# Batched matrix product on one core: a fourth output buffer, stores queued one pair later, and another order of copies on VectorE

## The chip, the cores and the metric

The kernel runs on one core of a Trainium2 chip. The core has engines that run side by side and meet only through semaphores: TensorE (PE, with its weight loads as PEld) multiplies and transposes, VectorE (DVE) and ScalarE (ACT) copy results out of the accumulators, GpSimd (POOL) and SyncE (SP) here mostly issue transfers. Sixteen DMA engines move data between the device memory (HBM) and the core's memory (SBUF); accumulators lie in PSUM. The metric is the device time of one execution in microseconds. Smaller is better.

## The reference

```python
def setup_inputs():
    batch, m, k, n = 32, 512, 1024, 768
    return {"x": randn(batch, m, k), "weight": randn(batch, k, n)}   # float32

def reference(x, weight):
    return np.matmul(x, weight).astype(np.float32)
```

There are 32 independent products of a 512 x 1024 by a 1024 x 768 matrix. All inputs are read once and all outputs written once, in float32: 167.77 MB in, 50.33 MB out.

## The kernel before

**Tiling.** TensorE contracts over 128 partitions, so x must lie transposed: K on the partitions. Each batch is handled as four row tiles (`mt` 0 to 3) of 128 rows; each needs 8 steps over K (`ko`) with 768 output columns. Loads go through POOL's queue and turn float32 into bfloat16 on the way (`load_w`, L89; `load_x`, L94). A weight load is one batch, an x load holds two batches, a "pair": batches 1 and 2, 3 and 4, and so on to 29 and 30. Batch 0 and batch 31 stand alone; batch 0's x comes in float32 through SP's queue into the space of an output buffer (`x_first`, L55).

**Transposes.** For a pair, TensorE does eight groups (`g`) of four transposes (L153) into two alternating accumulators `pts`, and VectorE copies each group into `both`, the transposed x (`spread_pair`, L222, its copy on L233; the last pair uses two smaller copies, L231 and L232; the last batch L236). Semaphore `s_pt` counts groups transposed, `s_c` groups copied. From the third group on, TensorE waits until the accumulator that it will overwrite has been copied.

**Multiplies and evictions.** `multiply` (L129) runs one row tile. Row tiles 0 and 1 share one set of three accumulator banks, 2 and 3 the other (`pms`). Each half batch (`p` 0 or 1) is copied out by two engines: ScalarE takes bank 0 and half of bank 2 (L265, L268; semaphores `s_a`, `s_ap`), VectorE bank 1 and the other half of bank 2 (L279, L281; `s_d`, `s_dp`). An output pair is batches 2a and 2a + 1; the two fill one output buffer `outs` of 24 KB per partition, and one store of 3 MB writes it (`store`, L107). The waits on `s_a` and `s_d` in `pair_on_pe` (L159) keep a multiply from overwriting a bank that isn't copied out: the second row tile of a batch waits for VectorE's bank 1 of the half batch just before it, as VectorE's order then also guarantees bank 2 of the half before that.

**What sets the order.** Each engine's program is one list, written out by hand: `on_pe`, `on_dve`, `on_act`, `on_pool`, `on_sp`. Transfers issued on one queue are moved in the order of issue.
- POOL issues, in round `b` of its loop (L321): for odd `b` the x load of the pair after next (which waits on `s_pt` until the old contents are transposed), then the store of output pair (b - 3) / 2; then for every `b` the weights of batch b + 3 (waits on `s_mm` until batch b - 1 is multiplied). In round 28 it issues the last two of its stores, 12 and 13.
- SP waits for every load's landing in the order of issue (`landed`, L298) and hands it on through `s_wr` (weights) and `s_xr` (x), which TensorE takes (L157). After all loads it issues the store of pair 14 and four half stores for batches 30 and 31.
- VectorE: for an odd batch first the eight copies of the pair's transposes; then, for every batch, the evictions of its two halves. So the second half of an even batch is evicted before the next pair's copies.
- Before an output buffer is written again, ScalarE and VectorE wait for its store (`slot_free`, L241). With three buffers, that is the store of three pairs ago.
- At the end SP waits for its stores, POOL for its own, and POOL clears the semaphores (`clear_on_pool`, L350).

Of the kernel before, what the change touches and what calls it, by code (L numbers as in the profile page):

```python
# [12 lines left out]
def kernel(  # L13
# [7 lines left out]
    B, M, K = x.shape  # L21
# [3 lines left out]
    MT = M // P  # L25
# [3 lines left out]
    ROW = MT * N  # L29
    AHEAD = 3  # L30
    LATE = 4
    HELD = 3
    GROUPS = 2 * MT
    W_SLOTS, X_SLOTS, OUT_SLOTS = 4, 2, 3
    LOOPS = (B - 4) // W_SLOTS
    LOOPED = 2 * LOOPS

    pe, dve, act, pool, sp = nc.tensor, nc.vector, nc.scalar, nc.gpsimd, nc.sync
# [7 lines left out]
    def sbuf(name, shape, dtype):  # L46
        return nc.alloc_sbuf_tensor(name, shape, dtype).ap()
# [4 lines left out]
    both = [sbuf(f"xT{i}", [P, 2, JT, 2, H, 2], BF16) for i in range(MT)]  # L52
    outs = [sbuf(f"out{i}", [P, 2 * ROW], F32) for i in range(OUT_SLOTS)]
    one = sbuf("one", [P, ROW], F32)
    x_first = outs[2][:, :MT * K].rearrange("p (mo k) -> p mo k", mo=MT)  # L55
    pts = [nc.alloc_psum_tensor(f"pt{i}", [P, JT, P], F32).ap() for i in range(2)]
    pms = [
        [nc.alloc_psum_tensor(f"pm{s}{i}", [P, 512], F32).ap() for i in range(3)] for s in range(2)
# [4 lines left out]
    def sem(name):  # L63
        sems.append(nc.alloc_semaphore(name))
        return sems[-1]

    s_first, s_zero, s_ident = sem("s_first"), sem("s_zero"), sem("s_ident")
    s_w = [sem(f"s_w{i}") for i in range(W_SLOTS)]
    s_x = [sem(f"s_x{i}") for i in range(X_SLOTS)]
    s_wr, s_xr = sem("s_wr"), sem("s_xr")  # L70
# [10 lines left out]
    def pt_done(k):  # L81
        return GROUPS * (k + 2)
# [6 lines left out]
    def load_w(b):  # L89
        if b >= W_SLOTS:  # L90
            pool.wait_ge(s_mm, mm_done(b - W_SLOTS))
        pool.dma_start(out=ws[b % W_SLOTS], in_=w_view[b]).then_inc(s_w[b % W_SLOTS], 16)  # L92

    def load_x(k):  # L94
        if k >= X_SLOTS:
            pool.wait_ge(s_pt, pt_done(k - X_SLOTS))
        slot = xs[k % X_SLOTS]
        if 2 * k + 1 == B - 1:
            pool.dma_start(out=slot[:, :MT], in_=x_view[B - 1]).then_inc(s_x[k % X_SLOTS], 16)
        else:  # L100
            pool.dma_start(out=slot, in_=pair_view[k]).then_inc(s_x[k % X_SLOTS], 16)  # L101
# [5 lines left out]
    def store(eng, a, sem):  # L107
        copied(eng, out_done(2 * a + 1) - 1)
        eng.dma_start(out=two_view[a], in_=outs[a % OUT_SLOTS]).then_inc(sem, 16)  # L109

    def store_half(b, p):
        src = one if b == B - 2 else outs[(b // 2) % OUT_SLOTS]
        half = slice(p * N2, (p + 1) * N2)
        copied(sp, 2 * b + p)
        sp.dma_start(out=out_view[b, :, half], in_=src[:, half]).then_inc(s_fin, 16)
# [106 lines left out]
    def spread_pair(k, g):  # L222

        pt = pts[g % 2].bitcast(BF16).rearrange("p j (b i r) -> p j b i r", b=2, r=2)
        tile, half = both[g // 2], g % 2
        if 2 * k + 2 == B - 2:

            rows = tile[:, 1].rearrange("p j h i r -> p j (h i r)").rearrange(
                "p j (m r) -> p j m r", r=2
            )  # L230
            dve.tensor_copy(tile[:, 0, :, half], pt[:, :, 0])  # L231
            return dve.tensor_copy(rows[:, :, half::2, :], pt[:, :, 1])  # L232
        return dve.tensor_copy(tile[:, :, :, half].rearrange("p b j i r -> p j b i r"), pt)  # L233
# [7 lines left out]
    def slot_free(eng, b):  # L241
        a = b // 2
        if a >= OUT_SLOTS and b % 2 == 0 and b < B - 2:
            eng.wait_ge(s_st[a % OUT_SLOTS], 16 * (a // OUT_SLOTS))
        if b == B - 1:
            eng.wait_ge(s_st[a % OUT_SLOTS], 16 * (a // OUT_SLOTS))

    def pieces(b, p, i):

        pm = pms[p][i]  # L250
        if b >= B - 2:
            dst = one if b == B - 2 else outs[(b // 2) % OUT_SLOTS]
            at = p * N2 + 512 * i
            return [(dst[:, at:at + 512], pm)]
        mine = outs[(b // 2) % OUT_SLOTS][H * (b % 2):H * (b % 2 + 1)]
        starts = [p * N2 + h * ROW + 512 * i for h in range(2)]
        return [(mine[:, at:at + 512], pm[H * h:H * (h + 1)]) for h, at in enumerate(starts)]

    def out_on_act(b, p):
        j = 2 * b + p  # L260
        if p == 0:
            slot_free(act, b)
        act.wait_ge(s_mm, 2 * j + 1)
        for piece in pieces(b, p, 0):
            last = act.copy(*piece)  # L265
        last.then_inc(s_a, 1)
        act.wait_ge(s_mm, 2 * j + 2)
        act.copy(*pieces(b, p, 2)[0]).then_inc(s_ap, 1)  # L268

    def out_on_dve(b, p):  # L270
        j = 2 * b + p
        if p == 0:
            slot_free(dve, b)
        dve.wait_ge(s_mm, 2 * j + 2)
        if b >= B - 2:
            dve.tensor_copy(*pieces(b, p, 1)[0]).then_inc(s_dp, 1)  # L276
            return
        for piece in pieces(b, p, 1):
            last = dve.tensor_copy(*piece)  # L279
        last.then_inc(s_d, 1)  # L280
        dve.tensor_copy(*pieces(b, p, 2)[1]).then_inc(s_dp, 1)  # L281

    def on_dve():
        for b in range(B):
            if b == 0 or b % 2:
                spread = {0: spread_first, B - 1: spread_last}.get(b)
                for g in range(MT if b == B - 1 else GROUPS):
                    dve.wait_ge(s_pt, (0 if b == 0 else pt_done(b // 2 - 1)) + g + 1)
                    (spread(g) if spread else spread_pair(b // 2, g)).then_inc(s_c, 1)
            for p in range(2):  # L290
                out_on_dve(b, p)

    def on_act():
        for b in range(B):
            for p in range(2):
                out_on_act(b, p)

    def landed(what, i):  # L298

        slots, ready = what  # L300
        sp.wait_ge(slots[i % len(slots)], 16 * (i // len(slots) + 1))
        sp.sem_inc(ready, 1)

    def on_pool():
        load_w(0)
        pool.memset(ident, 0.0).then_inc(s_zero, 1)
        pool.wait_ge(s_zero, 1)
        pool.affine_select(
            out=ident,
            in_=ident,  # L310
            compare_op=mybir.AluOpType.not_equal,
            fill=1.0,
            base=0,
            pattern=[[-1, P]],
            channel_multiplier=1,
        ).then_inc(s_ident, 1)
        load_x(0)
        load_w(1)
        load_w(2)
        load_x(1)  # L320
        for b in range(B):  # L321
            if b % 2 and b + AHEAD + 1 < B:
                load_x((b + AHEAD) // 2)
            if b % 2 and 2 < b < B - HELD - AHEAD:
                a = (b - 3) // 2
                store(pool, a, s_st[a % OUT_SLOTS])
            if b + AHEAD < B:
                load_w(b + AHEAD)
            if b == B - LATE:
                for a in (b // 2 - 2, b // 2 - 1):  # L330
                    store(pool, a, s_st[a % OUT_SLOTS])

    def on_sp():
        w, x = (s_w, s_wr), (s_x, s_xr)
        for what, i in ((w, 0), (x, 0), (w, 1), (w, 2), (x, 1)):
            landed(what, i)
        for b in range(B):
            if b % 2 and b + AHEAD + 1 < B:
                landed(x, (b + AHEAD) // 2)
            if b + AHEAD < B:  # L340
                landed(w, b + AHEAD)
        store_half(B - 2, 0)
        store(sp, B // 2 - 2, s_fin)
        store_half(B - 2, 1)
        store_half(B - 1, 0)
        store_half(B - 1, 1)
        sp.sem_inc(s_zero, 1)
        sp.wait_ge(s_fin, 80).then_inc(s_fin, -80)
# [10 lines left out]
    with tc.tile_critical():  # L359
        sp.dma_start(x_first, x_view[0]).then_inc(s_first, 16)  # L360
        on_pool()
        on_pe()
        on_dve()
        on_act()
        on_sp()
        clear_on_pool()
# [30 lines left out]
```

## Time and profile before

| | us |
|---|---|
| median of 3 runs | 515.88 |
| lowest and highest | 515.14, 516.1 |
| the profiled execution | 515.67 |
| its span, first to last instruction | 513.5 |
| PE busy | 430.2 (84%) |
| DVE busy | 209.6 (41%) |
| ACT busy | 110.2 (21%) |
| mean granted TensorE clock | 0.962 of full speed |

The views of the profile used here: the page's rows of busy tenths (one digit per fortieth of the span); the waits, with total, number and longest; the timeline, where a line gives start, duration, engine, source line, operation and in brackets the idle time before it with what ended it; the list of DMA issues, with size and time from issue to landing; and windows, which give each engine's busy time in a stretch and the share of time in which the DMA engines were busy. That share can come out a little over 1, as packets overlap. "L157" is line 157 of the kernel; "PEq" is TensorE's sequencer, "SPq" SP's.

A batch's multiplies take 10.35 us when TensorE waits for nothing. One eviction of half a bank takes VectorE 0.69 us, one copy of a transposed group 0.69, and ScalarE's copy 0.58.

### The profile page before, as it was taken

What the parts mean: (1) busy time and instruction counts of PE and PEld (TensorE: products, weight loads), DVE (VectorE), ACT (ScalarE), POOL (GpSimd) and SP (SyncE); (2) the same over time, 40 slices, a digit from 0 to 9 for tenths busy, and PEclk for the clock granted to TensorE, in tenths of its full rate; (3) what the DMA queues carried; (4) which work ended last, traced back from release to release, by engine and by line L of the source; (5) the groups of instructions that cost most, each with busy time, mean ns of one, the idle gap of its engine ahead of it and who ended that gap; (6) DMA issues with size and microseconds to landing.
All of it is one profiled execution on the core that took longest, in us unless ns stands there. A gap on an engine that the chain in (4) does not pass through costs nothing. (4 is left out here: it accounts for less than half of the span.)

```text
span 513.5 us, 6063 instructions
## 1 busy us (share of the span) xinstructions
PE 430.2 (84%) x2528; PEld 280.2 (55%) x2576; DVE 209.6 (41%) x332; ACT 110.2 (21%) x189; POOL 33.7 (7%) x68
## 2 busy tenths in 40 slices
PE   0889898998789789897878988788988879888995
PEld 0666565656456465554645655464565646556663
DVE  0463534535353353532534335263153632536331
ACT  0012223131122112222112221212213122121311
POOL 3001010101001010010100101001010010010000
PEclk9999999899998889999889999999899898898999
DMA  8999999999999999999999999999999999999995
GB/s 254 212 216 221 220 208 221 336 217 319 234 229 326 219 335 218 241 311 222 333 217 266 291 218 333 219 285 269 220 335 216 301 252 224 334 213 220 370 426 245
DMA packets 9803, 135.40 MB, mean 264 GB/s; under 512 B 1088, under 2 KB 1088, under 8 KB 1600
## 3 DMA queue, kind: packets, MB, share of 16 engines
q0 software_dynamic: 8928, 126.88, 96.1%
q1 hardware_dynamic: 864, 8.39, 4.1%
q8 instruction: 5, 0.08, 0.1%
q14 instruction: 6, 0.05, 0.0%
HBM read 167.77 MB, written 50.33 MB: 425 GB/s over the span
## 5 line engine op out<-in xcount | busy, mean ns | idle before, releaser
L134 PE MATMUL pm<-w,xT 128*128 128x256 bf16 (+1 forms) x2000 | 338.8, 328 | 32.8 <-PEq L157 29.9
L134 PEld LDWEIGHTS pm<-w,xT 128*128 128x128 bf16 x2048 | 202.2, 99 | 168.0 <-issue 40.8
L279 DVE COPY out<-pm 64x512 f32<-64x512 f32 x120 | 82.6, 689 | 252.4 <-PE pm L134 251.5
L265 ACT COPY out<-pm 64x512 f32<-64x512 f32 (+1 forms) x122 | 70.7, 580 | 300.6 <-PE pm L134 299.9
L153 PE MATMUL pt<-ident,x 128*128 128x128 f32 x496 | 87.3, 326 | 32.6 <-DVE xT L233 30.0
L153 PEld LDWEIGHTS pt<-ident,x 128*128 128x128 f32 x496 | 73.7, 210 | 45.6 <-DVE xT L233 39.3
L233 DVE COPY xT<-pt 128x1024 bf16<-128x1024 bf16 x112 | 73.5, 688 | 14.5 <-PE pt L153 13.8
L268 ACT COPY out<-pm 64x512 f32<-64x512 f32 (+1 forms) x62 | 35.8, 578 | 89.2 <-PE pm L134 89.2
L281 DVE COPY out<-pm 64x512 f32<-64x512 f32 x60 | 41.2, 686 | 0.0
L101 POOL DMA_DIRECT2D x<-in_x_dram x15 | 8.0, 532 | 274.0 <-PE pt L153 273.8
L92 POOL DMA_DIRECT2D w<-in_weight_dram x32 | 17.2, 538 | 125.6 <-PE pm L134 124.6
L153 PE MATMUL pt<-ident,out 128*128 128x128 f32 x32 | 6.9, 371 | 12.7 <-DMA out<-in_x_dram 12.5
L153 PEld LDWEIGHTS pt<-ident,out 128*128 128x128 f32 x32 | 5.3, 207 | 14.1 <-issue 12.5
L216 DVE CAST xT<-pt 128x256 bf16<-128x256 f32 x16 | 6.0, 441 | 14.4 <-PE pt L153 14.0
L109 POOL DMA_DIRECT2D out_dram<-out x14 | 7.5, 536 | 1.4 <-DVE out L281 1.3
L276 DVE COPY out<-pm 128x512 f32<-128x512 f32 x2 | 1.4, 692 | 9.0 <-PE pm L134 9.0
L276 DVE COPY one<-pm 128x512 f32<-128x512 f32 x2 | 1.4, 692 | 7.7 <-PE pm L134 7.7
L231 DVE COPY xT<-pt 128x512 bf16<-128x512 bf16 x8 | 3.4, 422 | 1.1 <-PE pt L153 0.9
L232 DVE COPY xT<-pt 128x512 bf16<-128x512 bf16 x8 | 3.3, 415 | 0.0
L236 DVE COPY xT<-pt 128x1024 bf16<-128x1024 bf16 x4 | 2.6, 684 | 0.2 <-PE pt L153 0.2
L265 ACT COPY one<-pm 128x512 f32<-128x512 f32 x2 | 1.2, 585 | 4.0 <-PE pm L134 4.0
L268 ACT COPY one<-pm 128x512 f32<-128x512 f32 x2 | 1.2, 585 | 4.0 <-PE pm L134 4.0
(8 smaller groups left out, 2.7 us busy)
## 6 DMA issues: line engine op xcount, KB each, us to landing
w<-in_weight_dram POOLq DMA_DIRECT2D x32, 1536.0 KB, 41.2
out_dram<-out POOLq DMA_DIRECT2D x14, 3072.0 KB, 36.5
x<-in_x_dram POOLq DMA_DIRECT2D x15, 2048.0 KB, 29.6
out_dram<-out SPq DMA_DIRECT2D x1, 3072.0 KB, 13.0
out<-in_x_dram SPq DMA_DIRECT2D x1, 2048.0 KB, 11.4
out_dram<-one SPq DMA_DIRECT2D x2, 768.0 KB, 9.3
out_dram<-out SPq DMA_DIRECT2D x2, 768.0 KB, 4.3
x<-in_x_dram POOLq DMA_DIRECT2D x1, 1024.0 KB, 23.2
```

The lines of the kernel that those rows point to most:

```text
L92: pool.dma_start(out=ws[b % W_SLOTS], in_=w_view[b]).then_inc(s_w[b % W_SLOTS], 16)
L101: pool.dma_start(out=slot, in_=pair_view[k]).then_inc(s_x[k % X_SLOTS], 16)
L109: eng.dma_start(out=two_view[a], in_=outs[a % OUT_SLOTS]).then_inc(sem, 16)
L134: last = pe.matmul(pm[bank][:, at:at + size], xT[:, ko // 2, :, ko % 2], w[:, ko, off:off + size], start=(ko == 0), stop=(ko == KT - 1),)
L153: last = pe.transpose(pts[g % 2][:, i, :], rows, ident)
L216: last = dve.tensor_copy(xT[:, 2 * (g % 2) + j].rearrange("p (h i) r -> p r h i", h=2), pt[:, 2 * j:2 * j + 2].rearrange("p r (i h) -> p r ...
L231: dve.tensor_copy(tile[:, 0, :, half], pt[:, :, 0])
L233: return dve.tensor_copy(tile[:, :, :, half].rearrange("p b j i r -> p j b i r"), pt)
L265: last = act.copy(*piece)
L268: act.copy(*pieces(b, p, 2)[0]).then_inc(s_ap, 1)
L279: last = dve.tensor_copy(*piece)
L281: dve.tensor_copy(*pieces(b, p, 2)[1]).then_inc(s_dp, 1)
```

## The change

Three things are done together.

First, there are four output buffers in place of three, and POOL issues the store of output pair (b - 5) / 2, in place of (b - 3) / 2, in an odd round b: each store stands one pair later among the loads. Rounds up to 25 issue stores 0 to 10 (before: 0 to 11), and after the last weights POOL issues stores 11, 12 and 13 (before: 12 and 13). A buffer's reuse moves by a pair as well. Batch 0's x uses the space of the fourth buffer, and the last batch uses the fourth too.

Second, VectorE defers the second half's eviction of an even batch until it has made the copies of the next pair's transposes.

Third, SP only hands on the weights' landings. ScalarE waits for an x load's landing between its two halves of each even batch and raises `s_xr`. The wait and the raising are one call in `landed` now.

```diff
-    HELD = 3
+    HELD = 4
     GROUPS = 2 * MT
-    W_SLOTS, X_SLOTS, OUT_SLOTS = 4, 2, 3
+    W_SLOTS, X_SLOTS, OUT_SLOTS = 4, 2, 4
...
-    x_first = outs[2][:, :MT * K].rearrange("p (mo k) -> p mo k", mo=MT)
+    x_first = outs[3][:, :MT * K].rearrange("p (mo k) -> p mo k", mo=MT)
...
     def on_dve():
         for b in range(B):
             if b == 0 or b % 2:
                 spread = {0: spread_first, B - 1: spread_last}.get(b)
                 for g in range(MT if b == B - 1 else GROUPS):
                     dve.wait_ge(s_pt, (0 if b == 0 else pt_done(b // 2 - 1)) + g + 1)
                     (spread(g) if spread else spread_pair(b // 2, g)).then_inc(s_c, 1)
-            for p in range(2):
-                out_on_dve(b, p)
+                if b:
+                    out_on_dve(b - 1, 1)
+            out_on_dve(b, 0)
+            if b % 2 or b == B - 1:
+                out_on_dve(b, 1)

     def on_act():
         for b in range(B):
-            for p in range(2):
-                out_on_act(b, p)
-
-    def landed(what, i):
+            out_on_act(b, 0)
+            if b % 2 == 0:
+                landed(act, (s_x, s_xr), b // 2)
+            out_on_act(b, 1)
+
+    def landed(eng, what, i):
         slots, ready = what
-        sp.wait_ge(slots[i % len(slots)], 16 * (i // len(slots) + 1))
-        sp.sem_inc(ready, 1)
+        eng.wait_ge(slots[i % len(slots)], 16 * (i // len(slots) + 1)).then_inc(ready, 1)
...
             if b % 2 and b + AHEAD + 1 < B:
                 load_x((b + AHEAD) // 2)
-            if b % 2 and 2 < b < B - HELD - AHEAD:
-                a = (b - 3) // 2
+            a = (b - 5) // 2
+            if b % 2 and 0 <= a < B // 2 - 1 - HELD:
                 store(pool, a, s_st[a % OUT_SLOTS])
             if b + AHEAD < B:
                 load_w(b + AHEAD)
             if b == B - LATE:
-                for a in (b // 2 - 2, b // 2 - 1):
+                for a in range(B // 2 - 1 - HELD, B // 2 - 2):
                     store(pool, a, s_st[a % OUT_SLOTS])

     def on_sp():
-        w, x = (s_w, s_wr), (s_x, s_xr)
-        for what, i in ((w, 0), (x, 0), (w, 1), (w, 2), (x, 1)):
-            landed(what, i)
         for b in range(B):
-            if b % 2 and b + AHEAD + 1 < B:
-                landed(x, (b + AHEAD) // 2)
-            if b + AHEAD < B:
-                landed(w, b + AHEAD)
+            landed(sp, (s_w, s_wr), b)
```

## The prediction

> **What bounds the kernel now.** I read the page first, then TensorE's waits, then the DMA landings of one cycle, then the last 60 us.
>
> ```profile
> DMA  8999999999999999999999999999999999999995
> HBM read 167.77 MB, written 50.33 MB: 425 GB/s over the span
> ```
>
> The 16 DMA engines are busy in all but the first and the last of 40 slices. Next, what TensorE waits for:
>
> ```profile
> PE pt L153 <- DVE xT L233: 30.0, 35, 1.9
> PE pm L134 <- PEq L157: 29.9, 13, 3.6
> ```
>
> Two waits share 60 us: transposes held by VectorE's copies (L233), and multiplies held by the "weights are in" semaphore (taken at L157). One pair shows how they alternate:
>
> ```profile
> 212.67 1.11 PE L153 MATMUL pt<-ident,x 128*128 128x128 f32 x8
> 215.64 1.35 PE L153 MATMUL pt<-ident,x 128*128 128x128 f32 x8 [1.87 <-DVE xT L233]
> 217.18 1.34 PE L153 MATMUL pt<-ident,x 128*128 128x128 f32 x8 [0.19 <-DVE xT L233]
> 218.71 1.35 PE L153 MATMUL pt<-ident,x 128*128 128x128 f32 x8 [0.19 <-DVE xT L233]
> 220.11 10.35 PE L134 MATMUL pm<-w,xT 128*128 128x256 bf16 x62
> ```
>
> The next batch then starts at 233.78, after 3.33 us of waiting for weights. The cycle's issues are an x load at 191.25, a store at 191.79, and weights at 192.31 and 201.76; they took, to landing:
>
> ```profile
> x<-in_x_dram POOLq DMA_DIRECT2D x1, 2048.0 KB, 27.7
> out_dram<-out POOLq DMA_DIRECT2D x1, 3072.0 KB, 34.4
> w<-in_weight_dram POOLq DMA_DIRECT2D x1, 1536.0 KB, 41.1
> w<-in_weight_dram POOLq DMA_DIRECT2D x1, 1536.0 KB, 39.0
> ```
>
> Issue plus duration gives landings at 218.95, 226.2, 233.4 and 240.8; the next x load (220.35 + 30.7) lands at 251.05. So transfers finish strictly in order of issue: a store takes the queue 7.25 us, a weight load 7.3, an x load 9.7 to 10.3, together 31.5 to 32 us per pair. The weights that landed at 233.4 are those TensorE got at 233.78. TensorE by itself needs 28.0 us per pair (transposes began at 31.09 and 59.13, before the queue caught up). DMA is the bound of the steady part, TensorE's waits are its shadow.
>
> The end is different. The last weights (issued 454.54) land at 481.8, 16 us before TensorE needs them; from 455.49 TensorE runs on without waiting for a load, to 508.4. Meanwhile the engines have stores 12 to 14 (numbered by pair) and four half stores of 768 KB. The last halves, issued at 503.99 and 509.12, took
>
> ```profile
> out_dram<-out SPq DMA_DIRECT2D x1, 768.0 KB, 5.2
> out_dram<-out SPq DMA_DIRECT2D x1, 768.0 KB, 3.3
> ```
>
> and the engines' load in that stretch (PE, PEld, DVE, ACT, POOL, clock, DMA share, GB/s):
>
> ```profile
> 490.00:500.00 10.00, 9.46 (x60) 6.53 (x61) 3.87 (x6) 1.75 (x3) 0.00 (x0) 1.00 1.01 432
> 500.00:505.00 5.00, 5.00 (x33) 3.05 (x32) 0.69 (x1) 1.17 (x2) 0.00 (x0) 1.00 0.82 349
> 505.00:508.00 3.00, 2.95 (x20) 1.77 (x19) 0.00 (x0) 0.58 (x1) 0.00 (x0) 1.00 0.66 272
> 508.00:513.50 5.50, 0.32 (x2) 0.00 (x0) 0.69 (x1) 0.58 (x1) 0.00 (x0) 0.86 0.36 146
> ```
>
> Only here does DMA run short of work: the last half waits for TensorE and lands alone at 512.4; 1.1 us of closing steps follow.
>
> **The change part by part.** *VectorE's order.* The transposes' copies no longer stand behind three evictions of 0.69 us. Of the 1.87 us stall the ordinary 0.19 stays: 1.68 us off each of 15 pairs, 25 us in all. The deferred evictions now hold TensorE's second multiply of the next batch (it waits for `s_d`). Here the copies end at 220.78; two evictions (1.39 us) would end at 222.17; the second multiply begins a quarter of 10.35 us after 220.11, at 222.7. Margin 0.5 us, so nothing is added; were it missed, the overrun would lie in front of a load wait anyway. In the steady part what comes late next is the same weights: TensorE arrives 1.7 us sooner and waits 5.0 us instead of 3.3. Worth there: nothing. In the last pair and the last batch nothing waits for loads, so TensorE's own end gains 1.92 - 0.19 (last pair) + 0.43 - 0.19 (last batch) = 2.0 us.
>
> *Store a pair later.* Bytes and transfers stay the same. With 11 instead of 12 stores ahead of them the loads from the third cycle on land 7.25 us earlier: the weights awaited at 455.17 at 447.9, the last ones at 474.6. TensorE's end becomes 508.4 - 7.25 - 2.0 = 499.1. Store 11 now follows the last weights, with 12 and 13, on POOL's queue; POOL passes only load issues (0.53 us each) with it, and nothing waits for those. Does the queue run dry early, without the store at 67.39? The x load that before went out at 95.68 goes out near 91; the work then queued ends at 113.7 (77.22 + 36.5) - 7.25 = 106.4. 15 us of backlog: no.
>
> *ScalarE hands on x loads' ends.* 16 semaphore waits move from SP to ScalarE, between its two evictions of an even batch; ScalarE idles 2.0 us there (rows of L265). Behind the wait stands the second eviction. x loads are issued two pairs ahead and land 25 to 31 us later. The tightest is the first: it lands at 25.7 (3.06 + 22.6), and ScalarE asks for it at 26.7, when the first evictions are done. Later ones have 2 us (the second lands at 50.4, asked for near 52.5) and more. Cost: nothing; were one late, TensorE would wait for that load itself.
>
> *Fourth buffer, later reuse.* A slot is free as long after its store as before (both move by a pair). The last batch now waits for store 11, due at 481.9, at about 491: nothing.
>
> *The sum.* After 474.6 the queues hold stores 11 to 14 and four halves. Check the rate on before: store 12 landed at 489.2 (455.08 + 34.1); two stores and three halves at 7.25 and 1.82 (a quarter) make 20.0 and an end at 509.2; measured 503.99 + 5.2 = 509.2. So the last-landing engine had no gap until then, and only the last half came loose: 512.4 against 509.2 + 1.8 = 511.0. Changed kernel: 474.6 + 4 x 7.25 + 4 x 1.82 = 510.9, the same by the other way round. TensorE's way, 499.1 + 0.76 to issue + 3.3, ends at 503: 8 us inside. So the span ends 1.35 us earlier: 512.15; with the 2.17 us between span and profiled time (515.67) this is 514.3. The profiled run stands 0.2 us under the median of 515.88, inside the runs' 0.96 us.
>
> Bounds of that gain. Upwards, if the mean engine decides and not the last: idle over the last windows is 5 x 0.18 + 3 x 0.34 + 5.5 x 0.64 = 5.4 us; less 1.1 closing and 1.5 latency of the last transfer (3.3 - 1.8) leaves 2.8. Downwards: POOL's queue and SP's now share the engines from 481 to 511, not only from 491 to 497. The window 490 to 500 (432 GB/s, two queues) against 480 to 490 (431, mostly one) says zero cost; one 1.6% below over 30 us would take 0.5. If POOL's stores end last, clearing the semaphores comes behind them: at most another closing, 0 to 1.1 us. I take 1.35, as it rests on landings of the last engine, and a semaphore needs all 16.
>
> [...]
>
> **The rivals.** (B) *No measurable change.* The filled gap is returned by the shared queues (0.5) and the late clear (up to 1.1): 515.0 to 516.0. For it: the bytes are the same, 97% of the span is already transfer, and an engine's odd delay (x loads vary by 0.6 us) weighs as much as the gain. Against: none of these costs shows in the 490 to 500 window.
>
> (C) *Slower.* Place: the closing 30 us, where two queues hold work on all engines at once and large and small packets alternate. At 4.5% loss of rate the 1.35 us are gone, at 8% (2.4 us) the kernel takes 516.7, slower by 0.2%. Before shows this mixture for only 6 us, where it costs nothing; that is the case against.
>
> (D) *TensorE's savings show.* Were transfers not the bound, 25 us would come off, to 490. Against: the landings, 7.3 us apart without a gap.
>
> **How the numbers follow.** 0.2% is 1.03 us, about what a measurement here can tell from no change. Forecast 0.60 (own range 512.8 to 514.8), B 0.30, C 0.08, D 0.02. Predicted is the forecast's 514.3. Low end 512.8 (gain 2.8); high end 516.5, which takes in B and part of C. Faster 0.60 + 0.02, same 0.30, slower 0.08.
>
> **What would show it.** TensorE's wait for L233 falls from 30.0 to under 8 us, its wait at L157 rises to about 55 (11 times 5). The first store goes out near 91 us; the last weights land near 474.6; TensorE ends near 499. The last half, issued near 500, takes some 11 us to land, and DMA share stays above 0.95 up to 508. A last landing at 509 to 511 confirms the sum. Wrong would be: a DMA share that dips between 500 and 508 with TensorE done (the rings had more slack than landings tell), landings more than 7.6 us apart at the end (rival C), or a `s_d` wait of over 0.3 us per pair in TensorE's rows.

## The result and the profile after

| | before | changed |
|---|---|---|
| median of 5 runs each | 515.44 us | 513.64 us |
| lowest and highest | 514.68, 516.1 | 513.3, 514.01 |
| profiled execution, its span | 515.67, 513.5 | 514.01, 512.2 |

The ratio is 0.9964 with a 95% interval of 0.9949 to 0.9978: the change takes 0.2 to 0.5% off. The spans of the two profiled executions differ by 1.3 us, as the sum had it; the medians differ by 1.8. In the experiments below, many more runs give the same size: the span's median is 513.0 us in 33 runs of the kernel before and 511.8 in 12 runs with the later stores alone.

First TensorE's waits in the changed kernel (total, number, longest, in us):

```profile
PE pm L134 <- PEq L157: 40.2, 13, 5.2
PE pt L153 <- DVE xT L233: 9.5, 42, 0.3
```

The wait for VectorE's copies fell from 30.0 to 9.5 us and its longest from 1.9 to 0.3. The wait for weights rose from 29.9 to 40.2. One cycle of the timeline shows both at once:

```profile
130.94 10.56 PE L134 MATMUL pm<-w,xT 128*128 128x512 bf16 x64 [2.69 <-PEq L157]
141.34 1.11 PE L153 MATMUL pt<-ident,x 128*128 128x128 f32 x8
142.76 1.35 PE L153 MATMUL pt<-ident,x 128*128 128x128 f32 x8 [0.30 <-DVE xT L233]
144.29 1.35 PE L153 MATMUL pt<-ident,x 128*128 128x128 f32 x8 [0.19 <-DVE xT L233]
145.82 1.35 PE L153 MATMUL pt<-ident,x 128*128 128x128 f32 x8 [0.18 <-DVE xT L233]
147.01 10.56 PE L134 MATMUL pm<-w,xT 128*128 128x512 bf16 x64
162.75 0.59 PE L134 MATMUL pm<-w,xT 128*128 128x512 bf16 x1 [5.18 <-PEq L157]
```

From the first transposes to the first multiply it is 5.7 us (before: 7.4), and what was won is waited for at the next weights.

The last weights go out at 445.12 and the last half store at 502.09 (timelines of POOL and SP); the issues with their durations to landing:

```profile
445.12 0.53 POOL L92 DMA_DIRECT2D w<-in_weight_dram  x1 [9.34 <-PE pm L134]
...
502.09 0.33 SPq L115 DMA_DIRECT2D out_dram<-out  x1
```

```profile
w<-in_weight_dram POOLq DMA_DIRECT2D x1, 1536.0 KB, 29.5
...
out_dram<-out SPq DMA_DIRECT2D x1, 768.0 KB, 9.0
```

So the last weights land at 474.6 and the last output at 511.1: the forecast's 474.6 and 510.9. The half that took 3.3 us alone now takes 9.0, behind others. The windows of the end (the columns before the last three are busy times of engines; then clock, DMA share and GB/s):

```profile
490.00:500.00 10.00, 10.00 (x65) 6.32 (x64) 2.66 (x5) 1.76 (x3) 0.00 (x0) 1.00 1.02 435
500.00:505.00 5.00, 1.28 (x8) 0.51 (x6) 0.69 (x1) 0.58 (x1) 0.00 (x0) 1.00 0.95 404
505.00:508.00 3.00, 0.00 (x0) 0.00 (x0) 0.00 (x0) 0.00 (x0) 0.00 (x0) 0.51 0.95 397
508.00:512.20 4.20, 0.00 (x0) 0.00 (x0) 0.00 (x0) 0.00 (x0) 0.00 (x0) 0.50 0.16 66
```

Where the DMA engines were busy 0.82 and 0.66 of the time, they are now busy 0.95, with TensorE done at 501.3. From 490 to 500, with two queues at work, they moved 435 GB/s, against 432 before: no price for sharing shows. In finer windows the share falls before the last landing:

```profile
507.00:508.00 1.00, 0.00 (x0) 0.00 (x0) 0.00 (x0) 0.00 (x0) 0.00 (x0) 0.50 0.80 332
508.00:509.00 1.00, 0.00 (x0) 0.00 (x0) 0.00 (x0) 0.00 (x0) 0.00 (x0) 0.50 0.41 172
```

The engines do not finish together: of the 16 landings that the trace has for the last store, the first stands at 508.0 and the last at 511.1 us (before: 512.2 and 512.4).

The page's chain of waits does not tell this. It still reads, for the changed kernel:

```profile
PE pm L134 9%; PE pt L153 1%; DVE xT L231 0%; DVE xT L232 0%; DVE xT L236 0%; DVE out L276 0%
```

It follows instructions back from the last one issued, and the last store's issue does hang on TensorE. That the store then stood in a queue is not in it. The experiments below ask which of the two ends the kernel.

### The profile page after: what moved, and what is told of

Same layout as the page of the kernel before. It is cut to its first block, busy times and chain, and to the rows that moved or that the text cites. A ratio compares the mean times of both kernels' runs of the same rounds, so it can differ in the third digit from the quotient of the medians.

```text
span 512.2 us, 6109 instructions
## 1 busy us (share of the span) xinstructions
PE 437.9 (85%) x2576; PEld 278.8 (54%) x2576; DVE 206.8 (40%) x332; ACT 110.2 (22%) x189; POOL 33.7 (7%) x68
## 5 line engine op out<-in xcount | busy, mean ns | idle before, releaser
L134 PE MATMUL pm<-w,xT 128*128 128x256 bf16 (+1 forms) x2048 | 356.2, 337 | 40.2 <-PEq L157 40.2
L134 PEld LDWEIGHTS pm<-w,xT 128*128 128x128 bf16 x2048 | 205.8, 101 | 186.2 <-issue 61.5
L233 DVE COPY xT<-pt 128x1024 bf16<-128x1024 bf16 x112 | 72.2, 687 | 61.0 <-PE pt L153 61.0
L153 PE MATMUL pt<-ident,x 128*128 128x128 f32 x496 | 80.0, 302 | 10.5 <-DVE xT L233 9.5
L153 PEld LDWEIGHTS pt<-ident,x 128*128 128x128 f32 x496 | 69.2, 209 | 21.8 <-DVE xT L233 17.4
L236 DVE COPY xT<-pt 128x1024 bf16<-128x1024 bf16 x4 | 2.6, 688 | 5.2 <-PE pt L153 5.2
```

The lines of the kernel that those rows point to most:

```text
L134: last = pe.matmul(pm[bank][:, at:at + size], xT[:, ko // 2, :, ko % 2], w[:, ko, off:off + size], start=(ko == 0), stop=(ko == KT - 1),)
L153: last = pe.transpose(pts[g % 2][:, i, :], rows, ident)
```

## The experiments

The theory: transfers in order of issue set the pace throughout. Before, the last half store came loose from that queue, as it waited for TensorE; the change closes this gap, and the copies' order is hidden. The main rival: TensorE's chain still ends the kernel, and the gain is its shorter path.

**One part at a time.** Only VectorE's order:

```diff
-            for p in range(2):
-                out_on_dve(b, p)
+                if b:
+                    out_on_dve(b - 1, 1)
+            out_on_dve(b, 0)
+            if b % 2 or b == B - 1:
+                out_on_dve(b, 1)
```

> Only VectorE's order is changed; stores and SP are those of the kernel before. My theory: transfers set the pace up to the last weights, so TensorE's saved 25 us vanish in waits for weights, but behind the last such wait (the weights that land at 455.2) TensorE gains 2.0 us, the last half store is issued near 507.1 instead of 509.1, and the end is the later of that plus 3.3 us (510.4) and the engines' backlog (511.0): 0.3 to 1.4 us less than before (the throttle may take some). So either part alone would fill the gap at the end. Rival: the gain is the stores' alone, this order is worth nothing: no difference (within 0.3 us).

Measured: 514.76 us against 514.97, ratio 0.9987 (0.9975 to 0.9998); span 512.8. The last half was issued at 508.35 in place of 509.12 and landed alone:

```profile
508.35 0.33 SPq L115 DMA_DIRECT2D out_dram<-out  x1
```

```profile
out_dram<-out SPq DMA_DIRECT2D x1, 768.0 KB, 3.3
```

That is 0.8 us earlier, within the expected range of 0.3 to 1.4 but short of its best. Behind the last wait for weights TensorE's stalls and gaps shrank by 2.5 us, but the multiplies right after this wait took 12.24 us where the kernel before took 10.56, and so took 1.7 back. (A stretch of 3.4 us at half clock would do this, an estimate from the eleven stretches of this length in the trace of the kernel before; the mean granted clock was 0.945 here and 0.962 there.) How much the order is worth by itself stays open. The ratio's interval reaches from 0.1 to 1.3 us less, so the rival's "within 0.3 us" is not excluded, and other traces with the old order and the old stores issue the last half as early as 508.75 (the third experiment's). What is shown is that TensorE's 20 us of saved stalls do not come off the time: its wait for weights rose to 44.6 us.

Only the fourth buffer and the later stores:

```diff
-    HELD = 3
+    HELD = 4
     GROUPS = 2 * MT
-    W_SLOTS, X_SLOTS, OUT_SLOTS = 4, 2, 3
+    W_SLOTS, X_SLOTS, OUT_SLOTS = 4, 2, 4
...
-            if b % 2 and 2 < b < B - HELD - AHEAD:
-                a = (b - 3) // 2
+            a = (b - 5) // 2
+            if b % 2 and 0 <= a < B // 2 - 1 - HELD:
...
-                for a in (b // 2 - 2, b // 2 - 1):
+                for a in range(B // 2 - 1 - HELD, B // 2 - 2):
```

> Only the fourth buffer and the later stores; VectorE's order and SP are those of the kernel before. My theory: the last weights land near 474.6, TensorE ends near 501 to 503, the last half store queues behind others and lands near 511: span 512.0 to 512.6, 1.0 to 1.8 us less than before, the same as the whole change. Rival (VectorE's order makes the gain): no difference from before. Rival (queues share the engines badly at the end): slower than the whole change by over 0.5 us.

Measured: 513.86 us against 514.97, ratio 0.9975 (0.9963 to 0.9987); span 511.9. TensorE's waits are those of the old order, its wait for weights is shorter, and the last half, issued at 501.47, queues just as in the whole change:

```profile
PE pt L153 <- DVE xT L233: 30.3, 37, 1.9
PE pm L134 <- PEq L157: 21.4, 10, 3.3
```

```profile
out_dram<-out SPq DMA_DIRECT2D x1, 768.0 KB, 9.3
```

The stores alone bring the whole change's span (511.9 against 512.2, just under the expected 512.0 to 512.6), with 30 us of stalls at the copies left in place. This excludes the rival that VectorE's order makes the gain, and no loss from shared queues shows.

Only the handing on of x loads (ScalarE waits between its halves of an even batch, SP hands on weights alone):

```diff
-            for p in range(2):
-                out_on_act(b, p)
+            out_on_act(b, 0)
+            if b % 2 == 0:
+                landed(act, (s_x, s_xr), b // 2)
+            out_on_act(b, 1)
...
```

> Only the handing on of x loads moves to ScalarE. My theory: ScalarE idles where the wait stands and x loads land long before, so the time is that of before, within 0.3 us. Rival (SP's list of waits delayed the weights' signal): TensorE's waits at the taking of weights shorten, 0.5 us or more less.

Measured: 514.67 us against 514.97, ratio 0.9989 (0.9976 to 1.0002), span 513.2 against 513.5. The interval holds no change, and 0.3 us is what the expectation allowed for; a gain of that size is neither shown nor excluded. The rival's sign, a shorter wait for weights, did appear in the one trace (24.4 us against 29.9), but TensorE worked some 4.7 us longer there (its waits are 5.1 us shorter in all, and its last multiply ends 0.4 us sooner), at a granted clock of 0.953 against 0.962, and a TensorE that arrives later waits less; so the sign does not decide.

**More work for TensorE at the end.** Both kernels multiply row tiles 0 and 1 of the last batch twice:

```diff
-    def multiply(b, mt):
+    def multiply(b, mt, told=True):
...
-        last.then_inc(s_mm, 1)
+        if told:
+            last.then_inc(s_mm, 1)
...
             pe.wait_ge(s_dp, j - 1)
+            if mt < 2:
+                multiply(b, mt, told=False)
             multiply(b, mt)
```

> The changed kernel, with row tiles 0 and 1 of the last batch multiplied twice: 5.2 us more for TensorE, the output is the same. My theory: TensorE is not on the path at the end any more; it ends near 506.5, the last half store is issued near 507.3 and lands no later than 511.6: at most 0.5 us more than the changed kernel (513.6 to 514.2). Rival (the chain of waits is right that TensorE ends last): 5.2 us more, 518.8.

> The kernel before, with row tiles 0 and 1 of the last batch multiplied twice: 5.2 us more for TensorE, the output is the same. My theory: in the kernel before TensorE does set the end (its last half store lands 3.3 us after issue, alone), so all of it shows: 5.0 to 5.3 us more, where the changed kernel took nothing. Rival (both kernels end on the engines' backlog): under 1 us more.

Measured: the changed kernel with 5.2 us more work took 513.68 us, ratio 0.9969 (0.9957 to 0.9981) to the kernel before, the same as without it. The kernel before with this work took 520.25 against 515.01, ratio 1.0106 (1.0074 to 1.0138): all 5.2 us. The timeline and list of issues of the padded changed kernel:

```profile
506.56 0.33 SPq L115 DMA_DIRECT2D out_dram<-out  x1
```

```profile
out_dram<-out SPq DMA_DIRECT2D x1, 768.0 KB, 4.0
```

4.0 us to landing is nearly the 3.3 of a half that finds the engines free: the padding used up the slack almost exactly (0.7 us are left). The rival that TensorE's chain ends the changed kernel falls here, and with it the reading of the chain of waits.

**Less to transfer at the end.** In both kernels the store of output pair 14, on SP's queue, writes an eighth of its columns:

```diff
-        eng.dma_start(out=two_view[a], in_=outs[a % OUT_SLOTS]).then_inc(sem, 16)
+        eng.dma_start(out=two_view[a][:, :n], in_=outs[a % OUT_SLOTS][:, :n]).then_inc(sem, 16)
...
-        store(sp, B // 2 - 2, s_fin)
+        store(sp, B // 2 - 2, s_fin, N)
```

(`n` is a new argument of `store`, by default the whole row.)

> The changed kernel, with the store of output pair 14 writing an eighth of its columns (seven eighths of that pair's output, 2.75 MB, are left out). My theory: the closing backlog of transfers sets the end, so 6.35 us of it go, until TensorE binds: its end at 501.3 + 0.76 + 3.3 + 1.1 closing = 506.5; 5 to 6 us less than the changed kernel. Rival (TensorE's chain ends it): no difference.

> The kernel before with the same seven eighths of pair 14's store left out. My theory: the last half store is issued at 509.1 whatever is queued before it, and lands 3.3 us later: 0 to 0.4 us less than before. Rival (its end is on the backlog too): 4 to 6 us less.

Measured: the changed kernel so cut took 507.61 us, 6.0 less than the changed kernel's 513.64 (another chip's runs; its ratio to the kernel before is 0.986, 0.9829 to 0.9891), span 505.6, 6.6 less. Its last half was issued at 501.21 and landed alone, after 3.3 us: with these transfers gone it is TensorE's chain that ends it, as expected. The kernel before so cut took 515.73 against 515.01, ratio 1.0014 (0.9995 to 1.0033): no less at all. Its last half was issued at 509.05 and took 3.3 us, as ever:

```profile
509.05 0.33 SPq L115 DMA_DIRECT2D out_dram<-out  x1
```

The two pairs of runs mirror each other. Before, TensorE's time at the end counts in full and transfer time not at all; after the change it is the other way round, until TensorE's chain ends the kernel again. The scatter of the runs fits: 12 and 10 runs of two variants that transfers end (later stores alone; the changed kernel with more work) lie within 0.6 and 0.8 us, 12 runs with the new order alone within 1.8, and 33 of the kernel before within 2.8. Why the runs that TensorE ends scatter more was not tried.

**Where VectorE's order would count.** Every store of a pair writes an eighth of its columns, in the kernel before and in the changed one:

```diff
-        eng.dma_start(out=two_view[a], in_=outs[a % OUT_SLOTS]).then_inc(sem, 16)
+        eng.dma_start(out=two_view[a][:, :N], in_=outs[a % OUT_SLOTS][:, :N]).then_inc(sem, 16)
```

> The kernel before, each store of an output pair writing an eighth of its columns (seven eighths of 15 pairs' output are left out). Transfers per pair fall from 31.5 to about 25.1 us, under TensorE's 28.0. My theory: TensorE now sets the pace, waits at the taking of weights go to a few us, and the span is about 31.1 + 15 x 28.03 + 13.3 + 5.2 = 470, plus 1 to 10 us of lower granted clock. Rival (something else than transfers holds the weights back): waits at L157 stay near 30 us and the span over 485.

> The changed kernel with the same stores cut to an eighth. My theory: the saved stall of 1.68 us per pair, hidden in the full kernel, shows here: about 31.1 + 15 x 26.5 + 13.2 + 5.2 = 447, plus 1 to 15 us of lower clock and of loads that are now close (25.1 us a pair against 26.5): 12 to 24 us less than the kernel before with small stores. Rival (VectorE's order is worth nothing even where TensorE sets the pace): under 4 us.

Measured: 481.05 us (span 478.5) with the old order, 450.22 (span 448.3) with the changes: 30 us apart, more than the 12 to 24 expected. The two differ in all three parts of the change, so which part makes the difference is read from the waits. TensorE's waits, first the kernel before, then the changed one:

```profile
PE pt L153 <- DVE xT L233: 29.2, 31, 1.9
...
PE pm L134 <- PEq L157: 1.1, 1, 1.1
```

```profile
PE pt L153 <- DVE xT L233: 9.4, 42, 0.3
PE pm L134 <- PEq L157: 2.0, 2, 1.1
```

With less to store, the waits for weights are gone in both: transfers had caused them. And the reordering is real: the stall behind the evictions falls from 1.9 to 0.3 us per pair and now counts in full. Most of the rest of the 30 us goes with TensorE's clock (below).

## Why the prediction was right

*What bounds the kernel.* Right, and now shown: with the pairs' stores cut, the waiting at the weights fell from 29.9 to 1.1 us in the kernel before and from 40.2 to 2.0 in the changed one, and the kernel before took 35 us less.

*Stores a pair later, and the sum.* Right in the mechanism and at both ends of the sum: last weights 474.6 (forecast 474.6), last output 511.1 (510.9), span 512.2 (512.15). In between, two steps missed and cancelled, which is luck: the third half (issued at 496.95, 11.0 us to landing) landed at 508.0 where the sum has 509.1, and the last half landed 3.1 us behind it, where the sum allows a quarter of a store, 1.82. Why the last engine took longer over the last half is not shown. (The gain itself is 1.4 or 1.5 us by the sum's two ways; 1.35 was taken.) Of the two bounds, the last engine's landing was the right one, and not the mean engine's idle time (gain 2.8): the mean share is down to 0.41 from 508 to 509, and the last landing comes at 511.1; the measured gain of 1.8 us between medians lies between the two, and its interval (1.1 to 2.6 us, from the ratio's) holds 1.35 and not 2.8. The predicted 514.3 stands 0.7 us over the median: the profiled run, at 514.01 the slowest of the five, had 1.8 us around its span instead of 2.17, and the others had spans of 511.5 to 511.9.

*VectorE's order.* "Worth there: nothing" was right for the steady part. No wait of TensorE for a deferred eviction appears among its waits, as forecast. The step left unsaid is that the two parts do not add: the later stores alone bring as much as the whole change, and what the order moves at the end (0.8 us in one trace) is then hidden behind the queue.

*TensorE's own end and waits* were mis-sized. Forecast were an end at 499.1, 55 us of waits at L157 and under 8 at L233; measured 501.3, 40.2 and 9.5. The 55 (11 times 5) does not agree with the forecast's own end: waits of 29.9 us, plus the 25 saved, less the 9 by which TensorE ends sooner, make 46. The first stall of a pair keeps 0.30 us, not the 0.19 assumed. One batch alone, whose multiplies took 13.33 us (at a granted clock of 0.79) in place of 10.56, costs more than the 2.2 us by which the end was missed:

```profile
448.22 13.33 PE L134 MATMUL pm<-w,xT 128*128 128x512 bf16 x64 [3.40 <-PEq L157]
```

The mean granted clock fell from 0.962 to 0.946, a cost that the forecast left out. (Part of this fall lies behind TensorE's last multiply, where a lower clock costs nothing: up to there it is 0.96 before and 0.95 after.) The lower clock lies in front of waits and in the slack at the end (501.3 + 0.8 to the issue + 3.3 alone is 505.4, against 511.1), so it cost no time. That slack was forecast at 8 us and is 5.7.

*The signs named.* The first store went out at 92.25 (forecast: near 91). The last half was issued at 502.09 and took 9.0 us (near 500, some 11). The DMA share was 0.95 up to 508, where more than 0.95 was named, and in the last microsecond of this it was 0.80. One sign of rival C appeared by its letter: the stores of POOL's queue landed at 481.9, 489.6 and 500.1, more than 7.6 us apart. The sign was badly chosen, as SP's stores moved in between and the rate did not fall.

*ScalarE's wait and the fourth buffer.* No cost appeared; a gain of a few tenths by the former stays open.

*The rivals.* (C), that shared queues slow the end, is refuted by 427 and 435 GB/s between 480 and 490 and between 490 and 500 (before: 431 and 432). (B) is excluded by the ratio's interval, narrowly: the runs' upper limit is 0.22% below no change. (D) happened only where stores were cut. The closing transfers ran at 397 to 435 GB/s from 480 to 508.

## What to carry to other kernels

Where transfers set the pace, look for the moments at which the queue has nothing to move: that was all that reordering compute or transfers could win here, 1.3 us of 513, and it could be worked out from landings before a line was changed. Work that can wait (stores) is best kept for the stretch where the loads are over and compute still runs. Whether compute or transfers end a kernel is not to be read from the chain of waits alone: add a few microseconds to one, take a few from the other, and see which counts.

## What was not expected of the hardware

TensorE's lower granted clock went with its stalls, also where the longest after start-up was 1.9 us: the mean was 0.968 with such stalls and 1.0 without. With cut stores, the old order stalls TensorE 1.9 us once per pair and has no other wait of note; the new order has no stall over 0.4 us between its start-up and its end but one wait of 0.9 us for weights. The page's rows of granted clock, in tenths, first the old order, then the new:

```profile
PEclk9999999899999999989999899999989899898999
```

```profile
PEclk9999999999999999999999999999999999999999
```

A mean of 0.968 over 478.5 us makes some 31 us at half speed: nine stretches of 3.4 us, the length that such a stretch has in the trace of the kernel before (an estimate). One pair shows what a stretch costs: from 91.20 to 120.13, where the transposes go on after their stalls, the old order takes 28.9 us (the clock from 91 to 120 is 0.94), and a pair with the same stall at full clock takes 28.0 (31.09 to 59.13 in the kernel before). By the waits, 21 of the 30 us are stalls that went (29.2 + 1.9 us against 9.4 + 0.7, the small figures being the last pair's); nine stretches at 0.9 us (taken from the one pair above) make another 8, and TensorE's busy time agrees: 427.3 us in the old order, 417.7 in the new. So the time that went with the stalls was more than their length. That the stalls cause the drops was not tried by itself (other work filled into the stalls, say). The clock records of the kernel before and of the changed one agree with it: up to TensorE's last multiply they hold eleven and nine stretches at half speed, of 3.4 or 6.8 us, and each begins 2.0 to 4.6 us after the start of a wait of TensorE of 1.86 us or more. But such waits also pass without one: eight of the kernel before's fifteen stalls of 1.9 us at the copies, and even a wait of 3.6 us for weights. What decides between them stays open. In the changed kernel all nine stretches follow waits for weights, of 2.4 to 5.2 us.
